# Building Q, FF and FB of a bidirectional recurrence from seven block products instead of eight

## The chip, the cores and the metric

The kernel runs on one core of a Trainium2 chip. The metric is the device time of one execution in microseconds (us), the median of several runs. The core has a matmul engine (PE, with its weight loads shown as PEld), a vector engine (DVE), an activation engine (ACT), a general engine (POOL), and SP, which here issues most of the transfers (DMAs) between DRAM and the on-chip memory (SBUF). Matmul results land in PSUM, which has 8 banks of 128 x 512 float32 values.

## What is computed

One layer of an encoder with 2048 tokens and width 1024. `h = RMSNorm(x)` is multiplied by a 1024 x 10240 matrix, whose ten column blocks of 1024 are named Q, FF, FB, I, GA, U, V, GB, MA and MB:

```
proj = h @ w_in
y_a = hgrn2(Q, FF, FB, I, GA)                    # 8 heads, chunkwise scans forward (FF) and backward (FB)
y_b = gelu(U) * (W_s @ layernorm(gelu(V)) + b) * silu(GB)
merged = sigmoid(MA) * (y_a @ w_proj_a) + sigmoid(MB) * (y_b @ w_proj_b)
out = rmsnorm(x + merged @ w_out) * final_norm_w
```

In branch A a head's state is 128 x 128. The forward scan runs over the tokens in order, the backward scan in reverse; `f = lb + (1 - lb) * sigmoid(z)` decays the state, `q = silu(Q)` reads it, `k = 1 - f` and `v = I` feed it. The two outputs are added and normalized per head.

## The kernel before

Every float32 matrix is split into two float16 parts (hi and lo) after scaling by a power of two, and one product of two such matrices is three matmuls (hi x hi, hi x lo, lo x hi) that accumulate in PSUM. There are two ways to build a projection:

- **Directly** (`mm3`, L212 to L218): for each of the 8 blocks of 128 along the inner dimension three matmuls. `proj_ch` gives 128 channels by 512 tokens (24 matmuls of 512 columns), `proj_tm` gives tokens by 256 channels (matmuls of 256 columns), `proj_wide` tokens by 512 channels. I, Q, FF, FB and V are built this way. Units of 256 columns (`halves`, L171 to L207) are loaded, squared for the scale, and split (tile `wsplit`).
- **By seven block products** (`seven`, L769; `mm12`, L821): tokens, inner dimension and channels are each cut in two, and seven products of block sums (Winograd's form of Strassen's scheme, `PRODUCTS`) replace eight. One product is 12 matmuls of 512 columns (L826). A group gives 256 channels for half of the tokens (p is the half): four tiles of 128 x 512. U, GB, MB, MA, GA and the three later projections are built this way. The weight blocks are made by `Make`: `load` (raw), `square`, `scale`, `sums` (four subtractions, L703) and `split` (four conversions on ACT, L729, and four on DVE, L730) into a tile `seven` of 1792 KB. The sums of x blocks (`x_parts`, `x_last`) go to tiles `xs`. Results leave PSUM by an ACT copy (L779) or, where a partial product is to be added, on DVE (L859).

The order of the work. `phase1` (L299) first normalizes and transposes x, 16 tiles of 128 tokens, into four tiles `xT`, with the first unit of I and the first head of Q beside it. Then it goes through the heads in pairs; for a head, first the forward scan over the four segments of 512 tokens, then the backward scan. For each segment a product of FF or FB is followed by `gla_operands` (L449: sigmoids on ACT; scans, decays and products on DVE; the scaled queries on POOL, L505), `gla_scores` (L512), `gla_states` (L563) and `gla_outputs` (L585). These four are staggered: while the products of one segment run, the scores, states and outputs of the one before are issued. The results go to DRAM (`o_d`).

`values` (L879) builds V and normalizes it. After its first products stands a branch (`tc.If`, L925) on a flag that says whether the recurrence left its numeric range; if it did, `exact` recomputes it. The sums of x blocks are made beside the remaining V products. Then `branch_b` (L998) builds U and GB and mixes positions, `merge_gates` (L1102) builds MB and MA by seven-block groups of both token halves side by side (the gate groups), `branch_a` (L1187) builds GA, and `final` (L1293) the rest. Beside the gate groups, the blocks of w_proj_a, w_out and of branch B's result are made one unit at a time in one buffer (`rt2`) and kept in DRAM. Their steps have fixed places in a list that counts products (`at`, L1162): a unit has 4 places, later 3.25, and a place is the time of one product of each of the groups that run side by side.

The framework orders the instructions of each engine by the order in the program and by when they are ready; `high_priority` moves some forward. Waits and reuse of buffers follow from the tiles: a pool with `bufs=2` gives two buffers to tiles of one name.

## Time and profile before

| | us |
|---|---|
| median of 3 runs | 2355.73 |
| lowest, highest | 2355.07, 2357.44 |
| span of the profiled execution | 2355.4 |

The profile shows one execution on the chip. Its span, from the first to the last instruction, is the time of that execution as far as the profile has it. In it the transfers moved 281.25 MB, 119 GB/s on the mean. In a table of groups, a row names the line of the kernel, the engine, the operation, the tile written and the tiles read, the shapes and the count; then busy us and the mean ns of one; then the engine's idle time just before these instructions and what ended it. In a timeline a row has start, duration, engine, line and operation, and in brackets the idle time before it. Durations of matmuls overlap, since the next begins while the last still drains.

### The profile page before, as it was taken

What the parts mean: (1) busy time and instruction counts of PE and PEld (TensorE: products, weight loads), DVE (VectorE), ACT (ScalarE), POOL (GpSimd) and SP (SyncE); (2) the same over time, 40 slices, a digit from 0 to 9 for tenths busy, and PEclk for the clock granted to TensorE, in tenths of its full rate; (3) what the DMA queues carried; (4) which work ended last, traced back from release to release, by engine and by line L of the source; (5) the groups of instructions that cost most, each with busy time, mean ns of one, the idle gap of its engine ahead of it and who ended that gap; (6) DMA issues with size and microseconds to landing.
All of it is one profiled execution on the core that took longest, in us unless ns stands there. A gap on an engine that the chain in (4) does not pass through costs nothing.

```text
span 2355.4 us, 33759 instructions
## 1 busy us (share of the span) xinstructions
PE 2311.8 (98%) x12880; PEld 1293.4 (55%) x12880; DVE 1544.7 (66%) x3033; ACT 1019.8 (43%) x1871; POOL 267.1 (11%) x507
## 2 busy tenths in 40 slices
PE   7999999999999999999999999999999999999998
PEld 5666866685668566544544554444445544444443
DVE  5686647764875587697655465677776654697754
ACT  6624333333243333433364456666565542254432
POOL 2222202220222021211000000000000000000111
PEclk9999999999999999999999999999999999999999
DMA  5201110011001000122332232576675674887643
GB/s 181 80 6 32 32 41 10 28 37 36 10 28 37 19 10 28 56 63 86 120 108 86 76 107 91 208 261 238 258 254 186 233 274 132 285 266 275 248 139 112
DMA packets 169629, 281.25 MB, mean 119 GB/s; under 512 B 10992, under 2 KB 105200, under 8 KB 162288
## 3 DMA queue, kind: packets, MB, share of 16 engines
q1 hardware_dynamic: 146272, 236.77, 30.0%
q10 hardware_dynamic: 23184, 42.22, 4.9%
q8 instruction: 104, 1.70, 0.3%
q14 instruction: 69, 0.57, 0.1%
HBM read 174.08 MB, written 104.86 MB: 118 GB/s over the span
## 4 chain that ended last, share of the span: by engine, by line
PE 51%; DVE 2%; DMA 2%; issue 1%; POOL 0%; ACT 0%; POOLq 0%; SPq 0%; DVEq 0%; ACTq 0%
PE bank L826 45%; PE pin L217 2%; PE pin L218 2%; PE pin L216 2%; PE px L1027 1%; DVE seven L730 1%; PE px L1255 1%; DMA raw<-mg 0%; DMA seven<-kept 0%; DVE tmp L649 0%; DMA zs<-ga 0%; DVE zs L859 0%; DVE zs L1467 0%; DVE zs L1445 0%; DMA out_dram<-zs 0%
## 5 line engine op out<-in xcount | busy, mean ns | idle before, releaser
L826 PEld LDWEIGHTS <-seven 128*128 128x128 f16 x5376 | 524.2, 98 | 626.1 <-issue 10.5
L826 PE MATMUL bank<-seven 128*128 128x512 f16 x2016 | 438.2, 380 | 4.8 <-DMA seven<-kept 2.1
L826 PE MATMUL bank<-xT,seven 128*128 128x512 f16 x1920 | 425.7, 379 | 0.3 <-DVE p2t L130 0.3
L826 PE MATMUL bank<-xs,seven 128*128 128x512 f16 x1440 | 320.7, 379 | 0.0
L216 PE MATMUL pin<-xT,wsplit 128*128 128x512 f16 x768 | 291.1, 379 | 0.2 <-ACT xT L281 0.2
L218 PE MATMUL pin<-xT,wsplit 128*128 128x512 f16 x768 | 291.1, 379 | 0.0
L217 PE MATMUL pin<-xT,wsplit 128*128 128x512 f16 x768 | 291.1, 379 | 0.0
L217 PE MATMUL pin<-wsplit,xT 128*128 128x256 f16 (+1 forms) x768 | 237.5, 309 | 2.4 <-DVE wsplit L205 2.1
L218 PE MATMUL pin<-wsplit,xT 128*128 128x256 f16 (+1 forms) x768 | 237.5, 309 | 2.3 <-DVE xT L282 2.0
L216 PE MATMUL pin<-wsplit,xT 128*128 128x256 f16 (+1 forms) x768 | 237.1, 309 | 0.4 <-ACT xT L281 0.4
L859 DVE SCALAR_TENSOR_TENSOR zs<-bank,us,zs 128x512 f32<-128x512 f32 x120 | 89.3, 748 | 105.2 <-PE bank L826 79.7
L779 ACT ACTIVATE zs<-bank,us 128x512 f32<-128x512 f32 x120 | 81.1, 682 | 118.1 <-PE bank L826 106.3
L867 ACT ACTIVATE zs<-zs 128x512 f32<-128x512 f32 x120 | 75.0, 625 | 121.7 <-DVE zs L859 112.5
L218 PEld LDWEIGHTS <-wsplit 128*128 128x128 f16 x768 | 75.1, 98 | 90.0 <-DVE wsplit L205 0.4
L217 PEld LDWEIGHTS <-wsplit 128*128 128x128 f16 x768 | 75.1, 98 | 77.5
L216 PEld LDWEIGHTS <-wsplit 128*128 128x128 f16 x768 | 75.3, 98 | 75.8
L505 POOL TENSOR_TENSOR q<-ff,e 128x512 f32<-128x512 f32 x64 | 71.8, 1122 | 371.6 <-DVE e L503 213.5
L730 DVE SCALAR_TENSOR_TENSOR seven<-raw,ws,seven 128x1024 f16<-128x1024 f32 x56 | 69.9, 1280 | 56.5 <-ACT seven L729 56.5
L458 ACT ACTIVATE fz<-pin,wus 128x512 f32<-128x512 f32 x64 | 43.8, 685 | 140.5 <-PE pin L218 140.3
L218 PEld LDWEIGHTS <-xT 128*128 128x128 f16 x768 | 75.4, 98 | 42.4 <-DVE xT L282 5.1
L779 ACT ACTIVATE zs<-bank,su 128x512 f32<-128x512 f32 x72 | 48.7, 680 | 112.7 <-PE bank L826 103.2
L462 DVE TENSOR_SCALAR fz<-fz,fb,fa 128x512 f32<-128x512 f32 x64 | 35.8, 559 | 93.2 <-ACT fz L458 93.2
(208 smaller groups left out, 3586.6 us busy)
## 6 DMA issues: line engine op xcount, KB each, us to landing
kept<-seven SPq DMA_DIRECT2D x16, 1792.0 KB, 8.5
seven<-kept SPq DMA_DIRECT2D x16, 1792.0 KB, 9.9
wraw<-in_w_in_dram SPq DMA_DIRECT2D x20, 1024.0 KB, 5.1
raw<-in_w_in_dram SPq DMA_DIRECT2D x40, 512.0 KB, 4.6
xt<-in_x_dram SPq DMA_DIRECT2D x16, 512.0 KB, 4.0
o_d<-ob SPq DMA_DIRECT2D x32, 256.0 KB, 2.3
v<-V SPq DMA_DIRECT2D x16, 512.0 KB, 3.5
vl<-v SPq DMA_DIRECT2D x32, 256.0 KB, 3.0
```

The costliest lines, as they stand in the source:

```text
L216: nc.tensor.matmul(ps, lh(k), rh(k), start=(k == 0), stop=False)
L217: nc.tensor.matmul(ps, lh(k), rl(k), start=False, stop=False)
L218: nc.tensor.matmul(ps, ll(k), rh(k), start=False, stop=(k == KT - 1))
L458: nc.scalar.activation(out=fz[:, 1:SEG + 1], in_=ps, func=AF.Sigmoid, scale=us)
L462: nc.vector.tensor_scalar(out=f, in0=f, scalar1=fb, scalar2=fa, op0=ALU.mult, op1=ALU.add)
L505: nc.gpsimd.tensor_tensor(out=q0.rearrange("p (m c) -> p m c", c=64), in0=ff.rearrange("p (m c) -> p m c", c=64), in1=e8.rearrange("p n b ...
L730: nc.vector.scalar_tensor_tensor(out=out[1], in0=src, scalar=s, in1=out[0], op0=ALU.mult, op1=ALU.subtract)
L779: self.reads["act"] = self.nc.scalar.activation(out=t, in_=ps, func=AF.Copy, scale=su)
L826: nc.tensor.matmul(ps, lhs(x, k), rhs(y, k), start=start and not (k or n), stop=k == 3 and n == 2, skip_group_check=True)
L859: self.reads["dve"] = self.nc.vector.scalar_tensor_tensor(out=more, in0=ps, scalar=su, in1=more, op0=ALU.mult, op1=ALU.add)
L867: self.nc.scalar.activation(out=out, in_=more, func=func)
L1027: nc.tensor.matmul(px[:, n, :], v[:, n, :], wsT[:, g, :], start=True, stop=True)
```

## The change

Q, FF and FB are built by seven-block groups. The order of the work becomes:

1. `front`: x is normalized and transposed as before. I is built in full by `proj_tm` (units 0 and 1 beside x, units 2 and 3 behind it) and stored in DRAM (`i_d`). The blocks and block sums of x are made here (`x_parts`, now with S3 too) and stored in DRAM (`x_d`, 16 blocks of 1 MB).
2. Beside the last unit of I and beside V, the blocks of 17 weight units are made (`plan_units`, `make`): Q, FF and FB in four units each, three units of MB, one each of U and GB. The subtractions run on POOL. Fifteen units go to DRAM (1792 KB each); those of Q and FF for the first pair of heads, made last, stay in SBUF.
3. `recurrence`: 24 groups for Q, FF, FB and three MB groups for token half 0 at the end, in nine phases that alternate between the halves of the tokens. Seven places in SBUF hold the blocks of x of one half; in the last group of a phase each place is refilled with the next half's block as soon as its product has read it. Weight blocks are fetched part by part. The scan work of the segments is queued and issued in steps between the products (`pump`, `step_on`). All groups use three PSUM banks.
4. The branch on the flag stands behind the recurrence, no longer inside V. Branch B begins with blocks that are in SBUF already and fetches the others; its first unit runs its groups one after the other.
5. `merge_gates` leaves out the three groups that were done in the recurrence.

Within the scan work three instructions of a segment move: f's scaling and the copy of 8 of its columns from DVE to ACT, and the product `ff * q` from DVE to POOL.

The diff, cut to its core:

```diff
-        w, U4 = self.w_in, range(4)
-        todo = []
-        for hp in U4:
-            todo += [(w, c + U * hp) for c in (C_I, C_Q, C_FF, C_FB)]
-        todo += [(w, C_V, 2), (w, C_V + 2 * U, 2)]
-        self.todo, self.made, self.hooks, self.reads = todo, [], [], {}
-        self.reads_first = True
+        w = self.w_in
+        self.todo = [(w, C_I + U * hp) for hp in range(4)] + [(w, C_V, 2), (w, C_V + 2 * U, 2)]
+        self.made, self.hooks, self.reads = [], [], {}
+        self.reads_first, self.ahead_of = True, 0
...
-    def phase1(self):
+    def front(self):
+            self.pg = E(tc.tile_pool(name="p_misc", bufs=1, space=PSUM, reuse_waits="tile"))
+            self.pin = E(tc.tile_pool(name="p_in", bufs=5, space=PSUM))
+            self.px0 = E(tc.tile_pool(name="p_x", bufs=2, space=PSUM))
+            self.wu = E(tc.tile_pool(name="wu", bufs=6))
+            self.xT = [self.xTp.tile([P, 2, 4, 2, SEG], F16, name="xT", tag="xT") for b in range(NSEG)]
+            with tc.tile_pool(name="g_i", bufs=3) as self.gi:
+                with tc.tile_pool(name="xrt", bufs=1) as self.xrt:
+                    with tc.tile_pool(name="xp", bufs=3) as self.xp, tc.tile_pool(name="nwb", bufs=2) as nwp:
+                        self.x_stage(nwp)
+                    self.i_stage(2)
+                self.rt = E(tc.tile_pool(name="rt0", bufs=3, side="right"))
+                self.plan_units()
+                self.i_stage(3)
+            self.decays()
+            self.patterns()
+            with tc.tile_pool(name="vw", bufs=3, side="right") as self.vw:
+                self.values()
...
+                self.i_pair(0, n, units[0])
+                if n == 1:
+                    units.append(self.unit(self.w_in, C_I + U, ahead=0))
+                if n >= 2:
+                    self.i_pair(1, n - 2, units[1])
+                if b >= 2:
+                    self.part(3)
+            for i, part in enumerate(((A11, A12), (A21, A22))[b % 2]):
+                nc.sync.dma_start(out=self.x_d[b // 2][part], in_=self.xT[b][:, i])
...
+        for n in range(8):
+            self.i_pair(hp, n, unit)
+            if hp == 2:
+                self.part(2)
+            else:
+                self.make(n - 9)
...
+            groups = []
+            for hp in range(4):
+                a, b = hp % 2, 1 - hp % 2
+                if hp == 0:
+                    groups.append([("q", 0, 0, 0, None), ("f", 0, 0, 1, None)])
+                groups.append([("q", hp, 1, a, ("b", hp)), ("f", hp, 1, b, ("q", hp + 1) if hp < 3 else ("mb", 0)),
+                               ("b", hp, 1, a, None)])
+                if hp < 3:
+                    groups.append([("q", hp + 1, 0, b, None), ("b", hp, 0, a, ("f", hp + 1)),
+                                   ("f", hp + 1, 0, a, None)])
+            groups.append([("b", 3, 0, 1, ("mb", 1)), ("mb", 0, 0, 0, ("mb", 2)), ("mb", 1, 0, 1, ("u", 0)),
+                           ("mb", 2, 0, 0, ("gb", 0))])
+            tail = None
+            for n, phase in enumerate(groups):
+                p, last = n % 2, n == len(groups) - 1
+                for m, (kind, hp, _, slot, after) in enumerate(phase):
+                    end = m == len(phase) - 1 and not last
+                    g = self.r_group(kind, hp, p, slot)
+                    done = partial(self.after, slot, after, p, end)
+                    if m == len(phase) - 2 and not last:
+                        self.x_fetch(1 - p, A11, self.spare)
+                    first = list(self.ORDER[:2])
+                    for i in self.ORDER[:2]:
+                        next(g)
+                        done(i)
+                        self.pump()
+                    if tail:
+                        next(tail[0])
+                        tail[1](6)
+                        self.pump()
+                    for i in self.ORDER[2:6]:
+                        next(g)
+                        done(i)
+                        self.pump()
+                    tail = g, done
+            next(tail[0])
+            tail[1](6)
+            while self.queue or any(self.pipe):
+                self.step_on(True)
+            self.X = [{c: self.slot_part(self.slot[p, c]) for c in self.PARTS} if p == 0 else {} for p in range(2)]
+            self.range_flag()
...
+    def after(self, slot, key, p, end, n):
+
+        if key and n in self.LOADS:
+            at = slice(*self.LOADS[n])
+            self.nc.sync.dma_start(out=self.ws[slot][:, :, at], in_=self.pre[key].d[:, :, at])
+        if end:
+            i = self.ORDER.index(n)
+            free = self.slot.pop((p, self.PARTS[i]))
+            if i < 6:
+                self.x_fetch(1 - p, self.PARTS[i + 1], free)
+            else:
+                self.spare = free
...
+        self.credit += 8 / 7 if ready < 5 else 3 / 2
+        while self.credit >= 1:
+            if not self.step_on(False):
+                self.credit = min(self.credit, 1.0)
+                break
+            self.credit -= 1
...
+    def step_on(self, drain):
+
+        if self.turn == 0:
+            new = None
+            if self.queue and self.queue[0]["z"] is not None:
+                new = self.queue.pop(0)
+            if new is None and not drain:
+                return False
+            if new:
+                self.operands(new)
+            if self.pipe[0]:
+                self.scores(self.pipe[0])
+            self.pipe = [new] + self.pipe
+        elif self.turn == 1:
+            g = self.pipe.pop()
+            if g:
+                self.outputs(g)
+        elif self.pipe[1]:
+            self.states(self.pipe[1])
+        self.turn = (self.turn + 1) % 3
...
-        nc.vector.tensor_scalar(out=f, in0=f, scalar1=fb, scalar2=fa, op0=ALU.mult, op1=ALU.add)
+        nc.scalar.activation(out=f, in_=kk, func=AF.Sigmoid)
         fs = self.sm.tile([P, 8], F32, name="fs")
-        lead = 0 if d == 0 else 63
-        nc.vector.tensor_copy(out=fs, in_=f[:, lead::64])
+        nc.scalar.activation(out=fs, in_=f[:, lead::64], func=AF.Identity, scale=fb, bias=fa)
...
-        nc.vector.tensor_tensor(out=ff, in0=ff, in1=q, op=ALU.mult)
+        nc.gpsimd.tensor_tensor(out=ff, in0=ff, in1=q, op=ALU.mult)
...
+        keys = [("mb", 0), ("mb", 1), ("mb", 2), ("u", 0), ("gb", 0), ("b", 0), ("b", 1), ("b", 2), ("b", 3),
+                ("q", 1), ("q", 2), ("q", 3), ("f", 1), ("f", 2), ("f", 3), ("f", 0), ("q", 0)]
+        cols = dict(mb=C_MB, u=C_U, gb=C_GB, b=C_FB, q=C_Q, f=C_FF)
+        self.pre, self.ws = {}, [None, None]
+        invs = self.c.tile([P, len(keys)], F32, name="invs")
+        for n, (kind, u) in enumerate(keys):
+            m = self.pre[kind, u] = self.make_w(self.w_in, cols[kind], u, self.rt)
+            m.to, m.adds = invs[:, n:n + 1], nc.gpsimd
+
+        def end(m, i, key):
...
+        todo = []
+        for n, w in enumerate(work):
+            todo += [(n - 1.8, w[0]), (n - 1.0, w[1]), (n, w[2]), (n + 0.8, w[3]), (n + 1.4, w[4])]
+        self.making = sorted(todo, key=lambda x: x[0])
+
+    def make(self, slot):
+
+        while self.making and self.making[0][0] <= (slot + 8) * 18 / 37 - 1.8:
+            self.making.pop(0)[1]()
+
     def values(self):
...
-        flag = self.range_flag()
-        with tc.If(flag > 0):
...
-                self.side_by_side([gate(p) for p in range(2)], slots)
+                self.side_by_side([gate(p) for p in range(2) if v > 2 or p], slots)
...
+            self.front()
+            self.recurrence()
+        flag = nc.values_load(self.flag[0:1, 0:1], min_val=0, max_val=1)
+        with tc.If(flag > 0):
+            self.exact()
```

615 lines of the change are left out of this document (358 added, 257 removed).

## Prediction, made before the changed kernel ran

> **What bounds the kernel now.** I read the page's engine shares and chain, then busy time by stage, then the groups of the stages that change.
>
> ```profile
> PE 2311.8 (98%) x12880; PEld 1293.4 (55%) x12880; DVE 1544.7 (66%) x3033; ACT 1019.8 (43%) x1871; POOL 267.1 (11%) x507
> ...
> PE 51%; DVE 2%; DMA 2%; issue 1%; POOL 0%; ACT 0%; POOLq 0%; SPq 0%; DVEq 0%; ACTq 0%
> ```
>
> PE is busy for 2311.8 of 2355.4 us, and no other engine holds over 2% of the chain. Busy time by stage follows (start:end, length, then PE, PEld, DVE, ACT and POOL busy, granted clock, DMA share, GB/s). The first row is the first 15 us of the second row's stage; then come the x blocks, the recurrence with Q, FF, FB and I, the V products, branch B, the merge gates, and the rest.
>
> ```profile
> 0.00:15.00 15.00, 3.45 (x14) 2.40 (x15) 5.47 (x16) 8.78 (x12) 4.47 (x20) 1.00 0.86 285
> ...
> 0.00:105.00 105.00, 89.27 (x651) 65.94 (x652) 61.53 (x112) 72.55 (x119) 26.72 (x66) 1.00 0.41 136
> 105.00:968.00 863.00, 851.28 (x5645) 579.75 (x5643) 596.08 (x1607) 294.77 (x694) 171.47 (x260) 1.00 0.09 28
> 968.00:1135.00 167.00, 165.51 (x782) 75.80 (x780) 120.75 (x186) 56.12 (x90) 22.79 (x44) 1.00 0.23 69
> 1135.00:1430.00 295.00, 295.00 (x1499) 150.95 (x1498) 163.54 (x250) 142.00 (x241) 3.61 (x21) 1.00 0.29 95
> 1430.00:1750.00 320.00, 319.42 (x1507) 145.06 (x1506) 223.73 (x334) 204.00 (x297) 11.26 (x32) 1.00 0.62 225
> 1750.00:2355.40 605.40, 591.33 (x2806) 275.90 (x2804) 379.04 (x546) 250.34 (x436) 31.26 (x84) 0.99 0.63 216
> ```
>
> Length less PE busy is PE's idle time: 15.7, 11.7, 1.5, 0, 0.6 and 14.1 us, together 43.6. The clock is full, so time can only come from fewer matmuls, and every new idle stretch of PE is paid in full. I sum against the span, 2355.4 us; the median of the runs, 2355.73, is 0.3 more, which I leave out.
>
> **What is removed.** Q, FF and FB are the products "pin<-xT,wsplit": 24 matmuls for each of 8 heads, 4 segments and 3 matrices, 2304 in all.
>
> ```profile
> L218 PE MATMUL pin<-xT,wsplit 128*128 128x512 f16 x768 | 291.1, 379 | 0.0
> ...
> L216 PE MATMUL pin<-xT,wsplit 128*128 128x512 f16 x768 | 291.1, 379 | 0.2 <-ACT xT L281 0.2
> ```
>
> The 379 ns overlap, so their sum is not PE's time. The spacing of starts is:
>
> ```profile
> 956.91 0.38 PE L216 MATMUL pin<-wsplit,xT 128*128 128x512 f16 x1
> ...
> 959.94 0.38 PE L218 MATMUL pin<-wsplit,xT 128*128 128x512 f16 x1
> ```
>
> Fourteen intervals in 3.03 us are 0.2164 us each. The seven-block form needs 24 groups (3 matrices, 4 column pairs, 2 token halves) of 7 products of 12 matmuls, 2016 in all. That removes 288 x 0.2164 = **62.3 us**, and PE's work becomes 2311.8 - 62.3 = 2249.5. I, V, the scans' own matmuls and the three merge-gate groups are moved, not changed in number. What remains to predict is idle time, stage by stage.
>
> **Start and x blocks.** The first product still waits for weights and the first x tiles: 15 - 3.45 = 11.6 us stay. Behind it 15.7 - 11.6 = 4.1 us were idle. The new stage adds half of the block sums (DVE and ACT, formerly beside V) while two I units instead of one I unit and a Q head run on PE, with two PSUM buffers for transposes. DVE had 61.5 and ACT 72.6 us in 105. Between 0 more and a doubling twice over (16), I take 8.
>
> **Making seventeen weight units beside I and V.** Each unit costs two ACT squares, four ACT and four DVE conversions, four subtractions (now on POOL), two loads of 512 KB and, for fifteen units, a store of 1792 KB.
>
> ```profile
> L687 ACT ACTIVATE tmp<-raw 128x1024 f16<-128x1024 f32 x56 | 58.5, 1047 | 14.3 <-DMA raw<-in_w_in_dram 11.0 <-DMA raw<-in_w_proj_b_dram 2.6 <-DMA raw<-in_w_proj_a_dram 0.7
> ...
> L729 ACT ACTIVATE seven<-raw,ws 128x1024 f16<-128x1024 f32 x56 | 61.4, 1137 | 3.4 <-DVE ws L135 3.2
> ...
> L729 ACT ACTIVATE seven<-tmp,ws 128x768 f16<-128x768 f32 x56 | 49.2, 924 | 0.0
> ...
> L505 POOL TENSOR_TENSOR q<-ff,e 128x512 f32<-128x512 f32 x64 | 71.8, 1122 | 371.6 <-DVE e L503 213.5 <-DVE ff L489 154.9 <-DVE fz L466 3.0
> ```
>
> ACT: 2 x 1.05 + 2 x 1.14 + 2 x 0.92 = 6.2 us a unit; POOL: 4 x 1.12 = 4.5. The cover is V, 768 x 0.2164 = 166 us, and the last I unit, 384 matmuls of 256 columns at half that spacing (an estimate), 42: together 208 us, 12 us a unit. The engines fit. Transfers are close: 17 x 1.05 + 15 x 1.84 MB and about 19 MB of V weights, I, V and x blocks are 64 MB, 310 GB/s.
>
> ```profile
> 1630.00:1680.00 50.00, 50.00 (x235) 22.73 (x234) 34.26 (x47) 28.26 (x39) 0.51 (x3) 1.00 0.69 258
> ...
> 2150.00:2200.00 50.00, 47.77 (x221) 21.49 (x220) 42.08 (x58) 21.09 (x38) 2.08 (x3) 1.00 0.93 330
> ```
>
> 258 GB/s cost PE nothing, 330 filled the engines to 0.93 with 2.2 us idle. The units of Q and FF that the recurrence needs first are made last, so any lag in making appears as a PE gap at the seam. Bounds: 1.5 (as V now) to 43 (64 MB at 258 GB/s take 248 us, 40 over the cover, plus a few). I take 8, nearer to the row at 330.
>
> **The recurrence.** It loses I (1152 matmuls of 256 columns in this window, 125 us) and 62 us, and gains the first Q head and three merge-gate groups (252 x 0.2164 = 54.5): 851 - 125 - 62 + 27 + 54 = 745 us of PE. Does DVE fit?
>
> ```profile
> L489 DVE TENSOR_TENSOR ff<-ff,q 128x512 f32<-128x512 f32 x64 | 44.3, 692 | 0.3
> ...
> L462 DVE TENSOR_SCALAR fz<-fz,fb,fa 128x512 f32<-128x512 f32 x64 | 35.8, 559 | 93.2 <-ACT fz L458 93.2
> L205 DVE SCALAR_TENSOR_TENSOR wsplit<-wraw,ws,wsplit 128x2048 f16<-128x2048 f32 x14 | 34.9, 2492 | 24.9 <-ACT wsplit L204 24.9
> ...
> L465 DVE COPY fs<-fz 128x8 f32<-128x8 f32 x64 | 13.0, 203 | 1.9
> ```
>
> These four groups (128 us) leave DVE: L489 goes to POOL, L462 and L465 to ACT, L205 to the front. In come the additions of partial products, three for each of 27 groups:
>
> ```profile
> L859 DVE SCALAR_TENSOR_TENSOR zs<-bank,us,zs 128x512 f32<-128x512 f32 x120 | 89.3, 748 | 105.2 <-PE bank L826 79.7 <-issue 13.3 <-PE px L737 12.0
> ```
>
> 596 - 128 + 81 x 0.748 = 529 us, 71% of 745. ACT, from 295, stays under 60%. Before, the stretches dense in scans already had DVE near 80%:
>
> ```profile
> 155.00:205.00 50.00, 50.00 (x309) 32.00 (x309) 38.48 (x103) 16.82 (x56) 15.41 (x20) 1.00 0.06 17
> 205.00:255.00 50.00, 48.82 (x309) 32.14 (x308) 39.24 (x113) 19.19 (x34) 6.87 (x13) 1.00 0.08 27
> ```
>
> There PE lost 0 and 1.2 us in 50. At that mean 745 us lose 9. Two things are worse: three product banks, whose tightest turn leaves one product (12 x 0.2164 = 2.6 us) to empty a bank, and POOL, whose instructions on two tiles double. They delay DVE:
>
> ```profile
> 172.71 0.42 DVE L560 TENSOR_TENSOR at<-at,ad 64x256 f32<-64x256 f32 x1
> ...
> 174.03 1.29 DVE L560 TENSOR_TENSOR at<-at,ad 64x256 f32<-64x256 f32 x1
> ...
> 174.00 1.04 POOL L505 TENSOR_TENSOR q<-ff,e 128x512 f32<-128x512 f32 x1 [4.85 <-DVE ff L489]
> ```
>
> The same instruction took 0.42 us alone and 1.29 beside POOL. The Trainium skill, page "SBUF — State Buffer", section "Who interferes with whom", says that a DVE instruction with two SBUF inputs and a POOL instruction that reads SBUF exclude each other for the whole instruction; these three rows agree. 64 more such meetings at 0.87 us are at most 56 us of DVE, which has 216 spare; PE sees a part. Bounds 9 to 68 (as if every meeting hit PE, 56, plus 12 as now); I take 25, because the 80% stretches already contain half of these meetings. Streaming x (8 x 7 blocks of 1 MB), weights and saved tiles is about 140 MB in 745 us, 190 GB/s, below the 258 that cost nothing. On SP's queue each fetch of an x block waits for the product that reads its place; behind it stand loads of I, of saved scores and of weight parts. Their users come three steps or a whole group (28 us with its scan work) later, so I cost this at nothing; without that cover it is one landing (5.2 us for 512 KB, below) at each of 8 changes of half, 42.
>
> **Drain and branch.** The last scan segment has no products beside it, and the branch on the range flag now stands with nothing behind it, where before V products covered it.
>
> ```profile
> 955.00:975.00 20.00, 17.58 (x120) 12.27 (x119) 14.09 (x38) 5.33 (x18) 9.64 (x11) 1.00 0.14 41
> ...
> 982.18 0.13 DVE L1493 TENSOR_SCALAR flag<-cnt 1x1 int32<-1x1 f32 x1
> ...
> 987.53 1.28 ACT L902 ACT_TABLE_LOAD   x1 [3.66 <-DVEq L925]
> ```
>
> The end of the scans cost 2.4 us with half its cover; without, I take 5 (0 to 8). From flag to ACT's first instruction behind the branch were 5.3 us, 3.7 of them waiting: I take 6 (3.7 to 10). Together 11.
>
> **Branch B and merge gates.** The first three gate steps have half the products, while making of the other weights beside them keeps its places: a place lasts 2.6 us instead of 5.2.
>
> ```profile
> L703 DVE TENSOR_TENSOR tmp<-raw 128x512 f32<-128x512 f32 x64 | 43.6, 685 | 10.6 <-ACT tmp L687 7.1 <-DMA raw<-in_w_out_dram 3.2
> ...
> raw<-in_w_proj_a_dram SPq DMA_DIRECT2D x8, 512.0 KB, 5.2
> ```
>
> One unit in its one buffer takes 5.2 us of load, 2.1 of squares, some 1.5 for the scale (an estimate), 4 x 0.685 of sums and 5 of conversions, 16 in all, against 4 x 2.6 = 10.4. Five units lag by up to 28 us; later places are 3.25 x 5.2 = 16.9 and the units there skip the squares, so they catch up. Bounds 0.6 to 28, taken with the loading of x's second half: 8.
>
> **Sum.** Idle: 11.6 + 8 + 8 + 25 + 11 + 8 + 14.1 (the end, unchanged) = 85.7. 2249.5 + 85.7 = **2335 us**, 20 less than now. Two thirds of the gain are given back at seams.
>
> **Rivals.**
> - All is hidden: old idle 43.6 plus 5 for the branch, 2298. For it: 98% busy in the old stages at equal DVE load; against it: the branch has lost its cover.
> - POOL's lock makes DVE the bound of the recurrence (slower). If all POOL work, 171 + 72 = 243 us, excludes DVE's 529, the scans need 772 us, and the first result is there only after some 11 products (29 us): 801 + 12 against 745 + 25, 43 over my sum, 2378. It decides when the recurrence idles over 25 + 20 = 45 us, 0.3 us a segment above my value. For it: the 1.29 us; against: the stretch with 38.5 us of DVE and 15.4 of POOL in 50, which kept PE at 50.00. The rule of the Trainium skill named above, taken to its end, is this case.
> - Transfers set the pace of making: 248 us instead of 208 + 8: 2367, slower too.
> - The change does nothing measurable: the give-backs reach 62. That the products are not fewer is excluded by the count above.
>
> **Chances.** My forecast (2315 to 2348) 0.50, hidden 0.20, lock 0.15, transfers 0.10, no difference 0.05. About 0.2% (4.7 us) is what a measurement can tell from no change: faster 0.70, same 0.05, slower 0.25. The range leaves out a little of the hidden case and the upper end of the lock: 2298 to 2374.
>
> **What would show it.** 288 fewer f16 matmuls of 512 columns, with Q, FF and FB on "bank"; PE idle of 20 to 30 us in that stage, with waits on DVE behind POOL; one PE gap of some 8 us between V and the recurrence, ended by a weight conversion, and one of about 11 us at the branch. Wrong would be: DVE over 90% in the recurrence, DMA share over 0.9 beside V, or no gap at the seams.

## The result and the profile after

The changed kernel takes 2374.4 us (median of 4 runs, 2370.6 to 2380.7) against 2355.4 us before (4 runs, one more than in the table above; 2355.1 to 2357.4): a ratio of 1.0079, 95% interval 1.006 to 1.0098. It is **0.8% slower** where 0.9% faster was forecast; 2374.4 lies 26 us above the forecast's 2315 to 2348 and just above the whole range, which ends at 2374. The profiled execution has a span of 2376.0 us.

Engine shares and the chain of the page of the changed kernel:

```profile
PE 2275.7 (96%) x12592; PEld 1275.6 (54%) x12592; DVE 1615.4 (68%) x2891; ACT 1158.7 (49%) x2105; POOL 447.9 (19%) x572
...
PE 19%; DMA 6%; DVE 5%; issue 3%; ACT 1%; POOL 0%; ACTq 0%; POOLq 0%; DVEq 0%; SPq 0%
```

The 288 matmuls are gone (12880 to 12592 instructions), yet PE's busy time fell by 36.1 us, not by 62.3, and PE's share of the chain fell from 51% to 19%: part of the rest now goes through DMA, DVE and issue, that is, through seams. Busy time by stage of the changed kernel follows (start:end, length, then PE, PEld, DVE, ACT, POOL busy, granted clock, DMA share, GB/s); the rows are the start, the x blocks, I and V with the making of units, the recurrence, the branch with branch B, the merge gates, the rest.

```profile
0.00:15.00 15.00, 3.53 (x14) 2.41 (x15) 5.37 (x16) 8.88 (x13) 3.49 (x16) 1.00 0.87 286
15.00:125.00 110.00, 96.20 (x835) 83.50 (x835) 92.89 (x127) 67.45 (x107) 21.88 (x34) 0.98 0.70 250
125.00:407.00 282.00, 263.54 (x1642) 157.95 (x1640) 160.71 (x233) 156.07 (x216) 119.85 (x127) 0.98 0.68 241
407.00:1169.00 762.00, 745.56 (x4532) 479.66 (x4531) 623.21 (x1435) 358.11 (x839) 249.11 (x258) 0.99 0.51 164
1169.00:1510.00 341.00, 333.17 (x1662) 167.84 (x1661) 168.31 (x260) 154.91 (x278) 10.34 (x27) 0.98 0.37 126
1510.00:1755.00 245.00, 228.15 (x1049) 101.99 (x1047) 175.51 (x264) 154.84 (x213) 11.38 (x26) 0.97 0.72 262
1755.00:2376.00 621.00, 605.52 (x2868) 282.21 (x2866) 389.38 (x559) 258.42 (x445) 31.88 (x84) 0.99 0.63 214
```

Length less PE busy is PE's idle time. The column before the DMA share is the clock, and it is below 1.00 in almost every stage; before, it was 1.00 in all but the last.

| stage | idle, forecast | idle, measured |
|---|---|---|
| start | 11.6 | 11.5 |
| x blocks | 8 | 13.8 |
| making beside I and V, with the seam | 8 | 18.5 |
| recurrence | 25 | 16.4 |
| drain and branch; branch B and merge gates | 11 + 8 | 7.8 + 16.9 |
| rest | 14.1 | 15.5 |
| **sum** | **85.7** | **100.3** |
| PE busy | 2249.5 | 2275.7 |
| span | 2335 | 2376.0 |

So the 41 us that are missing are 14.6 us of idle time and **26.2 us in which PE was busy for longer with the same matmuls**. That second part had no term in the forecast. It is seen where an idle stretch ends, in PE's timeline behind the first V products:

```profile
225.71 0.38 PE L217 MATMUL pin<-wsplit,xT 128*128 128x512 f16 x1
225.92 0.24 PE L191 MATMUL misc<-wsb,ones 128*128 128x1 bf16 x4
229.38 0.20 PE L919 MATMUL misc<-wsb,ones 128*128 128x1 bf16 x2 [3.21 <-DVE p2t L132]
233.12 1.44 PE L215 MATMUL pin<-wsplit,xT 128*128 128x512 f16 x3 [3.54 <-ACT wsplit L203]
234.36 0.63 PE L216 MATMUL pin<-wsplit,xT 128*128 128x512 f16 x1
234.78 0.63 PE L217 MATMUL pin<-wsplit,xT 128*128 128x512 f16 x1
```

Before the wait a matmul of 512 columns takes 0.38 us; after 3.21 and 3.54 us of waiting the same form takes 0.63, and starts are 0.42 us apart instead of 0.2164: half speed. Over the span the granted clock is 0.986, against 0.997 before: (1 - 0.986) x 2376.0 = 33 us of clock are withheld, before 7. The difference, 26, is the missing busy time. In the trace's record of the clock it comes in fourteen stretches at half clock, of 3.41 or 6.83 us but for the last, with 67.3 us in all; before there are three, with 12.2 us. Half of the difference is 27.5.

PE's waits in the changed kernel, by what released them (us in all, times, longest):

```profile
PE px L919 <- POOL wsb L869: 17.4, 7, 5.2
PE misc L919 <- DVE p2t L132: 11.1, 5, 5.2
PE pin L215 <- ACT xT L279: 10.0, 7, 3.0
PE pt L92 <- DVE am L90: 8.0, 1, 8.0
PE sc L713 <- POOL ff L670: 5.4, 5, 2.1
PE po L775 <- DVE fz L647: 5.2, 3, 1.7
PE bank L1009 <- PEq L1868: 4.8, 1, 4.8
```

The two longest are on L919, the matmul of one column that adds up the squares of a weight block for its scale. It stands in order in PE's queue: while its input or its bank isn't ready, no product behind it starts in these rows. The 11.1 us lie beside V, the 17.4 in the merge gates but for 2.0 in branch B. In the making, the longest of them looks like this (timeline, all engines):

```profile
325.78 4.50 DVE L912 SCALAR_TENSOR_TENSOR seven<-raw,ws,seven 128x1024 f16<-128x1024 f32 x2
...
327.07 2.12 POOL L881 TENSOR_TENSOR tmp<-raw 128x512 f32<-128x512 f32 x1
...
333.86 0.21 PE L919 MATMUL misc<-wsb,ones 128*128 128x1 bf16 x2 [5.20 <-DVE p2t L132]
```

Two conversions on DVE take 4.50 us beside a subtraction on POOL, and the tiny read that frees the scale matmul's bank stands behind them and three more on DVE, at 333.67 us. From this came two readings: that the matmul's place in the queue is the fault (**theory of the blocked queue**), or that DVE and POOL exclude each other and the making has no slack left (**the lock**). By the second, taking away one wait must bring it back at another place.

### The profile page after: what moved, and what is told of

Same layout as the page of the kernel before. It is cut to its first block, busy times and chain, and to the rows that moved or that the text cites. A ratio compares the mean times of both kernels' runs of the same rounds, so it can differ in the third digit from the quotient of the medians.

```text
span 2376.0 us, 34157 instructions
## 1 busy us (share of the span) xinstructions
PE 2275.7 (96%) x12592; PEld 1275.6 (54%) x12592; DVE 1615.4 (68%) x2891; ACT 1158.7 (49%) x2105; POOL 447.9 (19%) x572
## 5 line engine op out<-in xcount | busy, mean ns | idle before, releaser
L1009 PEld LDWEIGHTS <-seven 128*128 128x128 f16 x7392 | 725.8, 98 | 849.7 <-issue 38.4
L1009 PE MATMUL bank<-xT,seven 128*128 128x512 f16 x4116 | 939.1, 382 | 10.6 <-PEq L1868 4.8
L1043 DVE SCALAR_TENSOR_TENSOR zs<-bank,us,zs 128x512 f32<-128x512 f32 x192 | 142.1, 744 | 172.2 <-PE bank L1009 145.2
L670 POOL TENSOR_TENSOR ff<-ff,q 128x512 f32<-128x512 f32 x64 | 91.7, 1433 | 332.7 <-DVE ff L666 108.4
L865 ACT ACTIVATE tmp<-raw 128x1024 f16<-128x1024 f32 x80 | 83.8, 1048 | 67.1 <-DMA raw<-in_w_in_dram 50.0
L215 PEld LDWEIGHTS <-xT 128*128 128x128 f16 x768 | 75.8, 99 | 50.8 <-ACT xT L279 11.8
L911 ACT ACTIVATE seven<-raw,ws 128x1024 f16<-128x1024 f32 x80 | 87.7, 1137 | 31.4 <-DVE ws L137 17.0
L217 PEld LDWEIGHTS <-xT 128*128 128x128 f16 x768 | 75.8, 99 | 41.5 <-DVE xT L280 4.3
L216 PEld LDWEIGHTS <-xT 128*128 128x128 f16 x768 | 75.9, 99 | 35.5 <-issue 1.9
L760 DVE SCALAR_TENSOR_TENSOR st<-st,e,pu 128x128 f32<-128x128 f32 x240 | 82.4, 343 | 17.3 <-PE pu L752 11.6
L912 DVE SCALAR_TENSOR_TENSOR seven<-tmp,ws,seven 128x768 f16<-128x768 f32 x80 | 83.5, 1072 | 6.6 <-ACT seven L911 6.1
L1043 DVE SCALAR_TENSOR_TENSOR zs<-bank,su,zs 128x512 f32<-128x512 f32 x72 | 53.8, 747 | 48.2 <-PE bank L1009 38.3
```

The costliest lines, as they stand in the source:

```text
L215: nc.tensor.matmul(ps, lh(k), rh(k), start=(k == 0), stop=False)
L216: nc.tensor.matmul(ps, lh(k), rl(k), start=False, stop=False)
L217: nc.tensor.matmul(ps, ll(k), rh(k), start=False, stop=(k == KT - 1))
L670: nc.gpsimd.tensor_tensor(out=ff, in0=ff, in1=q, op=ALU.mult)
L760: nc.vector.scalar_tensor_tensor(out=sn, in0=st, scalar=e8[:, n, last:last + 1], in1=pu[:, n, :], op0=ALU.mult, op1=ALU.add)
L865: self.nc.scalar.activation(out=junk[:, 1024 * h:1024 * h + 1024], in_=self.raw[:, h], func=AF.Square, accum_out=self.ss[:, h:h + 1])
```

## Experiments

All times are medians beside runs of the kernel before on the same chip, and ratios are to those, with their 95% interval; the changed kernel stands at 1.0079.

### One wait at a time in the front

The constants of the decays, which include an Exp, moved ahead of the last I unit:

```diff
+                self.decays()
                 self.rt = E(tc.tile_pool(name="rt0", bufs=3, side="right"))
...
-            self.decays()
             self.patterns()
```

> Against the changed kernel (2374.4 us), the constants of the decays (one DVE-ACT-DVE chain with an Exp) are computed before the last I unit and not between I and V. Theory of the blocked queue: the wait at 226 us (6.75 us of PE idle, then 6.8 us at half clock, which cost 3.4) is the scale matmul of a weight block, which stands in PE's queue and waits for DVE, which waits for that Exp; it goes, time 8 to 10 us less, some 2365, granted clock 0.986 to 0.988. Rival of the lock (POOL's subtractions slow DVE) and rival of transfers: the wait stays with another releaser, time unchanged within 3 us.

Measured: 2373.9 us, 1.0070 (1.0056 to 1.0083). Two rows of PE's timeline of this kernel:

```profile
334.29 0.21 PE L919 MATMUL misc<-wsb,ones 128*128 128x1 bf16 x2 [6.42 <-DVE p2t L132]
...
406.96 3.60 PE L1009 MATMUL bank<-xT,seven 128*128 128x512 f16 x8 [2.61 <-DVE seven L912]
```

The gap at 226 us shrank from 6.75 to 3.4 us, and the next one, at 328, grew from 5.20 to 6.42. Two PSUM banks for the scale matmuls:

```diff
-            self.pg = E(tc.tile_pool(name="p_misc", bufs=1, space=PSUM, reuse_waits="tile"))
-            self.pin = E(tc.tile_pool(name="p_in", bufs=5, space=PSUM))
+            self.pg = E(tc.tile_pool(name="p_misc", bufs=2, space=PSUM, reuse_waits="tile"))
+            self.pin = E(tc.tile_pool(name="p_in", bufs=4, space=PSUM))
```

> Against the changed kernel, the scale matmuls of the front get two PSUM banks instead of one, and the products of I and V four instead of five. Theory of the blocked queue: the waits of the scale matmul on the reading of its bank (11.1 us on DVE L132 in the whole kernel, at 226, 328 and 347 us) go, and with them one or two stretches at half clock: 8 to 14 us less, 2360 to 2366; what stays at 226 is the wait for V's weights, about 3.5 us. Rival of the lock: DVE is late anyway, so the idle time moves to the next conversion: within 3 us of the changed kernel. Four banks for products costs under 2 us by either.

Measured: 2373.6 us, 1.0070 (1.0057 to 1.0084). The wait of L919 on p2t left the table of waits; in its place stand

```profile
PE pin L215 <- ACT wsplit L203: 5.1, 1, 5.1
...
PE misc L919 <- POOL wsb L869: 3.8, 2, 2.1
PE pin L215 <- ACT V L1117: 3.8, 1, 3.8
PE bank L1009 <- ACT seven L911: 3.8, 1, 3.8
```

which are 16.5 us; in the changed kernel the row on p2t and the rows of these names have 11.1 + 3.5 + 1.2 = 15.8. Neither edit changed the time, and both expectations of the blocked queue failed: the waits are where lateness shows, not where it arises.

### The subtractions on DVE

```diff
-            m.to, m.adds = invs[:, n:n + 1], nc.gpsimd
+            m.to = invs[:, n:n + 1]
```

> Against the changed kernel, the 68 subtractions of the seventeen units made beside I and V run on DVE instead of POOL. Rival of the lock: conversions of L912 fall back to their 1.28 us (raw) and 1.01 us (tmp), the gaps at 328 and at 402 us close: 8 to 15 us less. Theory of the blocked queue: DVE gains 68 x 0.69 = 47 us of work in a queue on which the scale matmuls wait; the conversions are shorter but stand behind the subtractions: idle time of the front the same or up to 10 us more, 2372 to 2385.

Measured: **2362.6 us, 1.0024** (1.0014 to 1.0034). The rival won. Groups of 105 to 418 us, first of the changed kernel, then of this one (count | busy, mean ns of one):

```profile
L912 DVE SCALAR_TENSOR_TENSOR seven<-raw,ws,seven 128x1024 f16<-128x1024 f32 x34 | 49.3, 1477 | 10.1 <-ACT seven L911 9.6
L881 POOL TENSOR_TENSOR tmp<-raw 128x512 f32<-128x512 f32 x34 | 48.9, 1437 | 1.5 <-DMA raw<-in_w_in_dram 0.3
```

```profile
L912 DVE SCALAR_TENSOR_TENSOR seven<-raw,ws,seven 128x1024 f16<-128x1024 f32 x34 | 42.6, 1279 | 6.2 <-ACT seven L911 6.0
...
L881 DVE TENSOR_TENSOR tmp<-raw 128x512 f32<-128x512 f32 x34 | 23.3, 687 | 17.6 <-ACT tmp L865 17.1
```

A subtraction takes 0.69 us on DVE and 1.44 on POOL, and DVE's conversions are back at 1.28. The stage from 125 to 407 us of this kernel:

```profile
125.00:407.00 282.00, 270.98 (x1690) 162.09 (x1688) 189.43 (x308) 160.19 (x220) 30.77 (x63) 0.99 0.72 254
```

DVE and POOL together held 160.7 + 119.9 = 280.6 of 282 us in the changed kernel; here it is 220. The sum of 280.6 is no sign of a lock that fills the stage: laid over each other in the trace, the two are busy at once for 63.7 us, and for 65 us neither is. What the run shows is that POOL's part in the making set its pace: the time falls by 11.8 us when DVE gets *more* work, while two edits on the waits do nothing. It does not show by which way. A subtraction on POOL takes 1.27 us with nothing on DVE beside it (26 of the 68), against 0.69 on DVE, so each unit's chain was longer by itself; and where they meet they delay each other, POOL's 68 subtractions by 11.7 us together and DVE's conversions by 11.6. The edit takes away both, and no run separates them.

### Both front edits, and the order of the first V products

The two diffs of the decays and of the subtractions, together:

> Both front edits at once: subtractions of the units on DVE and the decays before the last I unit. Each alone: 11.8 us less and nothing. Theory of the pace (beside I and V the making is paced by DVE and POOL excluding each other, so a single wait taken away comes back at the next unit): with the pace gone, the wait at 226 us is no longer given back, so its 5.9 us of idle and some 3.4 us of half clock go as well: 2353 to 2358. Rival of the blocked queue (every wait stands by itself): the sum of the two single effects, 2360 to 2363.

Measured: 2362.6 us, 1.0019 (1.0009 to 1.0030), the same as the subtractions alone. This is the range of the rival, the sum of the single effects (2360 to 2363), though both theories had counted on the wait going. The gap at 226 us stayed at 6.0 us, with waits of the same names as before: the scale of V's second weights is read on DVE behind the subtractions of a unit, and its conversion stands on ACT behind that unit's. So no step of the making was left between the first two V products:

```diff
             norm(t, 0, product(t, 0))
-            self.make(t)
         wv[1] = self.unit(self.w_in, C_V + SEG, ahead=0)
```

> Subtractions on DVE, decays early, and no step of the making between the first two V products, so that the conversion of V's second weights doesn't stand behind those of a unit on ACT and DVE. Theory: the 6 us of idle at 226 us and its 6.8 us at half clock go and, since the pace no longer binds, don't come back: 2351 to 2357. Rival (the pace still binds with 211 us of DVE): the gap moves to 393 us, the seam to the recurrence, 2360 to 2365.

Measured: 2363.6 us, 1.0031 (1.0021 to 1.0042); the gap is 5.2 us. The time is in the rival's range, but the gap didn't move to the seam with the recurrence as the rival had it: the wait there is 2.2 us with and without this edit. So the mechanism was missed by both. Subtractions of a unit begun earlier still stand on DVE ahead of V's scale. This seam isn't mended by any run here.

### Places in the merge gates

```diff
-                    at = 3 + 4 * e if e < 4 else 15 + 13 * (e - 3) // 4
+                    at = (4, 10, 16, 22, 25, 28, 30, 33, 36, 38, 41, 44, 46, 49, 52, 54)[e]
```

> Against the changed kernel, the sixteen weight and z units of the merge gates stand at places of equal time (a place beside one gate alone is half as long): 4, 10, 16, 22, 25 ... 54 instead of 3, 7, 11, 15, 18 ... 54. Theory of the blocked queue: the four waits of the scale matmul at 1514 to 1577 us (9.9 us of idle, with 3.4 us or more at half clock) go, 8 to 12 us less. Rival: the units are paced by their one buffer (14.4 to 15.6 us from conversion to conversion, 16 of them in 236 us of products), so the wait only moves to the end of the merge gates, where 6.6 us are idle now: within 3 us of the changed kernel.

Measured: 2374.1 us, 1.0075 (1.0061 to 1.0089): the rival. The waits of L919 on POOL fell from 17.4 to 7.5 us, and this stood at the end of the stage:

```profile
1757.98 2.19 ACT L911 ACTIVATE seven<-raw,wos 128x1024 f16<-128x1024 f32 x2 [7.72 <-DMA kept<-seven]
...
1762.50 5.71 PE L1009 MATMUL bank<-xs,seven 128*128 128x512 f16 x15 [8.91 <-ACT zs L962]
```

ACT waits 7.72 us until the block before is stored (1792 KB from the one buffer), and the copy that empties a product's bank stands behind it. The changed kernel shows the pace of these units in its own timeline:

```profile
1714.35 2.19 ACT L911 ACTIVATE seven<-raw,wos 128x1024 f16<-128x1024 f32 x2 [1.19 <-DMA kept<-seven]
...
1729.99 2.19 ACT L911 ACTIVATE seven<-raw,wos 128x1024 f16<-128x1024 f32 x2 [5.48 <-DMA kept<-seven]
```

These two are 15.6 us apart; over ten such steps, from 1596 to 1744 us, it is 14.8 on the mean. Sixteen units at that pace are 236 us, and the products there, 13 half gates of 84 matmuls, last 13 x 84 x 0.2164 = 236 as well. The forecast's "later units catch up" has no room to happen.

### The merge-gate groups back

```diff
...
-            groups.append([("b", 3, 0, 1, ("mb", 1)), ("mb", 0, 0, 0, ("mb", 2)), ("mb", 1, 0, 1, ("u", 0)),
-                           ("mb", 2, 0, 0, ("gb", 0))])
+            groups.append([("b", 3, 0, 1, ("u", 0))])
...
-                self.side_by_side([gate(p) for p in range(2) if v > 2 or p], slots)
+                self.side_by_side([gate(p) for p in range(2)], slots)
```

> One part of the change undone: the three merge-gate groups of the first token half go back from the end of the recurrence into the merge gates. Theory of the pace: the merge gates get back 54 us of products to cover sixteen units, so their 16.5 us of idle time and three or four stretches at half clock (6 to 8 us) go; the end of the recurrence loses its cover and idles by the scans left in the queue, 20 to 35 us; together 2370 to 2388. Rival (the idle time of the merge gates has nothing to do with cover, it is the order of the queue): merge gates idle as now, 2390 to 2410.

Measured: 2387.7 us, 1.0123 (1.0106 to 1.0140), within the range of the theory of the pace. Windows of this kernel, the end of the scans with the branch, and the merge gates:

```profile
1085.00:1162.00 77.00, 51.01 (x318) 44.39 (x318) 59.53 (x138) 27.37 (x96) 34.84 (x36) 0.82 0.21 61
...
1500.00:1800.00 300.00, 299.06 (x1413) 136.31 (x1412) 207.39 (x307) 186.08 (x260) 10.54 (x28) 1.00 0.66 242
```

The merge gates idle for 0.9 us in 300: with the old cover their idle time is gone. The end of the scans with the branch (4.6 us) idles for 26 us, at a clock of 0.82. So the groups do cover the end of the scans; but in the changed kernel the last 149 us of the recurrence are full (148.7 us of PE), which leaves the question whether two would do. With the front as in the last run on it (2363.6 us):

```diff
-            groups.append([("b", 3, 0, 1, ("mb", 1)), ("mb", 0, 0, 0, ("mb", 2)), ("mb", 1, 0, 1, ("u", 0)),
-                           ("mb", 2, 0, 0, ("gb", 0))])
+            groups.append([("b", 3, 0, 1, ("mb", 1)), ("mb", 0, 0, 0, ("gb", 0)), ("mb", 1, 0, 1, ("u", 0))])
...
-                self.side_by_side([gate(p) for p in range(2) if v > 2 or p], slots)
+                self.side_by_side([gate(p) for p in range(2) if v > 1 or p], slots)
```

> The same, and one of the three merge-gate groups (the third of the first half) back in the merge gates. Theory of cover: the merge gates get 18 us more of products, their 16 us of idle and 7 to 10 us of half clock go; the end of the recurrence keeps two groups of cover and idles 5 to 9 us, with 3 of half clock: 8 to 14 us less than the run beside it, 2340 to 2348. Rival (cover at the end of the recurrence is worth the same): no difference.

Measured: **2350.8 us, 0.9970** (0.9958 to 0.9982), 12.8 us less than without it and faster than the kernel before. The difference is as forecast; the time is above 2340 to 2348, since part of the idle time stayed. Windows of this kernel:

```profile
1120.00:1150.00 30.00, 22.23 (x152) 16.19 (x151) 18.02 (x36) 9.77 (x42) 12.50 (x15) 0.92 0.41 118
...
1480.00:1740.00 260.00, 252.82 (x1184) 114.29 (x1183) 187.19 (x279) 166.53 (x228) 10.37 (x26) 0.99 0.71 259
```

The merge gates idle for 7.2 us instead of 16.9 in the changed kernel and 17.6 in the run without this edit, and the drain and the branch together for 7.8 of 30, as the branch and what follows it did with three groups.

### Block sums of x

In the version with one group back:

```diff
                 if b >= 2:
-                    self.part(3)
+                    self.part(2)
```

> The same as the run before it, with two steps instead of three of the block sums of x after each second x tile from the third segment on; the rest of them runs beside the third I unit. If the 14 us of idle in the x blocks (9 on ACT's copies of transposes) come from the block sums on DVE and ACT: 3 to 6 us less. If they are the rhythm of the tiles themselves: no difference.

Measured: 2354.0 us, 0.9989 (0.9979 to 0.9999), no gain over the run before it; PE's wait on ACT's copies of transposes is 11.5 us instead of 10.1. A third of the steps taken away from this place changes nothing, which speaks against the sums as the cause of the idle x blocks; what the cause is stays open.

### The clock, by itself

In the kernel before, pauses of PE in branch B and the merge gates (with 1 or 5 powers):

```diff
+    def pause(self):
+        nc, pt = self.nc, self.px()
+        nc.tensor.matmul(pt[:, 0, 0:1], self.ones16, self.gapb, start=True, stop=True)
+        nc.vector.tensor_copy(out=self.gapt[:, 2:3], in_=pt[:, 0, 0:1])
+        for _ in range(5):
+            nc.gpsimd.tensor_tensor(out=self.gapt[:, 1:2], in0=self.gapt[:, 2:3], in1=self.mhalf, op=ALU.pow)
+        nc.gpsimd.tensor_copy(out=self.gapb, in_=self.gapt[:, 1:2])
+        nc.tensor.matmul(pt[:, 1, 0:1], self.ones16, self.gapb, start=True, stop=True)
```

> The kernel before (2355.7 us) with fourteen pauses of TensorE in branch B and in the merge gates, 36 us apart: a tiny matmul, a read on DVE, one power on POOL (0.88 us), a cast and a second tiny matmul that waits. Nothing else changes. Theory of the clock: a pause of 1.5 to 2 us costs its own length only, 14 x 1.8 = 25 us, 2378 to 2385, granted clock stays at 0.997. Rival (any pause slows the clock): 14 x 1.7 to 3.4 us more and a clock of 0.98.

> The same with five powers in each pause, 5 to 6 us. Theory of the clock: each pause costs its length and then 1.7 to 3.4 us at half clock (3.4 to 6.8 us of half clock each): 14 x (5.5 + 2.5) = 112, some 2467, granted clock 0.96 to 0.985. Rival (half clock is only recorded, the time after a pause is the same): 14 x 5.5 = 77, some 2433.

Measured: 2376.3 us, 1.0084 (1.0066 to 1.0101), and 2442.5 us, 1.0365 (1.0347 to 1.0383). There are sixteen pauses and not fourteen (PE has 32 instructions more, two for each), and they came out shorter than planned, about 1 and 3.2 us; so both times lie below their forecasts. For the short ones, a pause in PE's timeline and PE's share:

```profile
1242.54 0.16 PE L849 MATMUL px<-gapb,ones 128*128 128x1 bf16 x1 [1.02 <-POOL gapb L848]
```

```profile
PE 2313.2 (97%) x12912; PEld 1293.1 (54%) x12912; DVE 1541.5 (65%) x3051; ACT 1020.6 (43%) x1871; POOL 285.2 (12%) x539
```

For the long ones the same, and the two stages with pauses up to 1740 us, with fourteen of them:

```profile
1255.14 0.16 PE L849 MATMUL px<-gapb,ones 128*128 128x1 bf16 x1 [3.05 <-POOL gapb L848]
```

```profile
PE 2345.4 (96%) x12912; PEld 1303.4 (53%) x12912; DVE 1540.1 (63%) x3051; ACT 1020.3 (42%) x1871; POOL 321.7 (13%) x603
```

```profile
1135.00:1430.00 295.00, 276.07 (x1344) 138.38 (x1343) 145.07 (x228) 130.99 (x225) 22.80 (x55) 0.95 0.28 90
1430.00:1740.00 310.00, 283.95 (x1306) 128.48 (x1305) 182.76 (x290) 164.07 (x243) 37.50 (x78) 0.96 0.47 174
```

Short pauses: the span grows by 2373.2 - 2355.4 = 17.8 us, 16.4 of them idle, 1.4 busy; the clock stays at 0.999. Long pauses: the span grows by 86.7, of which 96.7 - 43.6 = 53.1 are idle and 2345.4 - 2311.8 = **33.6 are matmuls at half clock**, with a mean clock of 0.984. Had half clock been on record only, as the rival has it, the span would have grown by the 53.1 alone. Fifteen of the sixteen long pauses, of 2.7 to 3.4 us, have a stretch at half clock behind them, none of the short ones has. By sixteen, a pause of 3.2 us costs 5.4 (86.7 / 16), one of 1 us costs 1.1. The Trainium skill, page "TensorE: Matmul & The Clock Gate", section "Part 1: The HAM clock gate", says that the array falls to half its clock after an idle window of about 3.4 us and needs a busy window of that length to return; the pauses agree in kind, and they already do it at 3.05 us.

### ff x q on DVE

```diff
-        nc.gpsimd.tensor_tensor(out=ff, in0=ff, in1=q, op=ALU.mult)
+        nc.vector.tensor_tensor(out=ff, in0=ff, in1=q, op=ALU.mult)
```

> Against the changed kernel (2374.4 us), the 64 products ff x q of the scans go back from POOL to DVE; the front is left as it is. Rival of the lock in the recurrence (POOL's products slow DVE there as its subtractions did beside I and V): DVE's groups in that stage get shorter, the waits on ff and on DVE (15 us of idle with two or three stretches at half clock) shrink: 8 to 15 us less. Theory of the pace (only the making is so dense that DVE and POOL exclude each other, 305 of 313 us; the recurrence has 620 + 252 of 762 us with the overlap left over): DVE takes 64 x 0.69 = 44 us more, the waits on POOL's ff (5.4 us) go and come back as waits on DVE: within 5 us, 2369 to 2379.

Measured: 2367.9 us, 1.0040 (1.0026 to 1.0054), 6.5 us less: between the two forecasts (8 to 15 less by the lock, at most 5 by the pace). Groups of the scans, of the changed kernel and then of this one:

```profile
L670 POOL TENSOR_TENSOR ff<-ff,q 128x512 f32<-128x512 f32 x64 | 91.7, 1433 | 332.7 <-DVE ff L666 108.4 <-DVE e L684 104.5 <-DVE ff L668 61.5
L677 DVE TENSOR_TENSOR kt<-zs,w 128x256 f32<-128x256 f32 x128 | 86.5, 697 | 0.0
...
L679 DVE TENSOR_TENSOR kt<-kt,fend 128x256 f32<-128x256 f32 x64 | 38.9, 608 | 0.0
```

```profile
L677 DVE TENSOR_TENSOR kt<-zs,w 128x256 f32<-128x256 f32 x128 | 58.5, 459 | 0.0
L670 DVE TENSOR_TENSOR ff<-ff,q 128x512 f32<-128x512 f32 x64 | 45.8, 716 | 0.2
L679 DVE TENSOR_TENSOR kt<-kt,fend 128x256 f32<-128x256 f32 x64 | 31.2, 487 | 0.0
```

The product of keys that DVE issues right behind the scan takes 459 ns on the mean with ff x q on DVE and 697 with it on POOL. DVE's busy time in the whole kernel is 1598.3 us here against 1615.4, **17.1 less although it does 45.8 more**: on POOL, ff x q cost DVE 62.9 us by waiting, more than DVE needs to do it. Then the same in the version with one merge-gate group back, and q0 with it:

```diff
-        nc.gpsimd.tensor_tensor(out=q0.rearrange("p (m c) -> p m c", c=64),
+        nc.vector.tensor_tensor(out=q0.rearrange("p (m c) -> p m c", c=64),
```

> The version with one merge-gate group back (2350.8 us) and ff x q on DVE. Theory of the lock in the recurrence: the 6.5 us of the single edit come again, 2342 to 2346, DVE's busy time falls by some 17 us. Rival (the single edit's gain was a draw of half clock in the front): 2349 to 2353.

> The same and q0 = ff x e on DVE as well, so that POOL holds no large product in the recurrence. Theory of the lock: one DVE instruction waits for most of each of POOL's 64 products of 1.1 us, so POOL's saving is already paid by DVE; DVE's busy time rises by less than 20 us instead of 64 x 0.69 = 44, and the time is within 4 us of the run beside it. Rival (q0 on POOL costs DVE nothing, since it comes at the end of the operands): DVE gains 44 us, waits on ff and on q0 get longer, 5 to 15 us slower than the run beside it.

Measured: **2341.1 us, 0.9937** (0.9923 to 0.9951), and 2344.5 us, 0.9941 (0.9927 to 0.9954). The pages of the two:

```profile
PE 2263.0 (97%) x12592; PEld 1271.0 (54%) x12592; DVE 1623.5 (69%) x3023; ACT 1157.8 (50%) x2103; POOL 273.6 (12%) x440
...
PE 27%; DVE 3%; DMA 3%; issue 2%; POOL 0%; ACT 0%; ACTq 0%; SPq 0%; POOLq 0%; DVEq 0%
```

```profile
PE 2266.5 (97%) x12592; PEld 1274.5 (54%) x12592; DVE 1625.7 (69%) x3087; ACT 1158.3 (49%) x2103; POOL 198.1 (8%) x376
```

ff x q gives 9.7 us here. DVE's time falls by 18.2 us, as it did alone. q0 adds 43.7 us of work to DVE and 2.2 us to its busy time: what q0 on POOL saved DVE, DVE had lost by waiting almost in full. The time doesn't change: 3.4 us more, with intervals that overlap.

## Why the prediction was wrong, step by step

- **"The clock is full, so ... every new idle stretch of PE is paid in full."** This is the step that failed, and it decided the sign. The clock was full because PE in the kernel before, behind its start, has two waits of little over 2 us (2.21 and 2.10, each with half clock behind it) and no longer one. In the changed kernel it has thirteen, of 2.15 to 5.20 us, and half clock costs 26.2 us more than before. With the measured idle time and the old clock the span would have been 2249.5 + 100.3 = 2349.8, faster by 0.24%. The pauses put into the kernel before show the mechanism without the change: 33.6 us lost at half clock with sixteen pauses of some 3.2 us. None of the forecast's own signs of being wrong came (DVE is at 82% in the recurrence, the DMA share beside V is 0.68, the gaps at the seams are there); the clock was not among them.
- **62.3 us removed** holds. Where the clock is nearly back (the fastest version, 2341.1 us, with 2263.0 us of PE at 0.991) 13.5 us over 2249.5 are left; PE's instructions are 12592 in both.
- **Making, 8 us: mis-sized, 18.5.** The seam was forecast as one gap ended by a weight conversion. Such a gap is there, at 402 us, with 3.8 us; the others stand within V. The forecast compared ACT and POOL, each by itself, with 12 us of cover a unit; it didn't sum DVE's part and treated POOL and DVE as independent. POOL's 4 subtractions were costed at 4 x 1.12 us and took 4 x 1.44. Taking them off POOL gave 11.8 us; how much of that is POOL's own length in each unit's chain and how much its meetings with DVE stays open.
- **Transfers at 310 GB/s** were named as the danger of that stage. With the subtractions on DVE the same stage moves more, 254 GB/s instead of 241, and idles less: transfers did not set its pace.
- **Recurrence, 25 us: mis-sized, 16.4.** The price of ff x q on POOL for DVE was bounded at 56 us and is 62.9; q0, which was on POOL before, costs it 41.5 (43.7 less 2.2), and DVE is busy for 623 us there instead of 529. What PE sees of it is little, because DVE still has 139 us to spare: 6.5 to 9.7 us. The 9.7 are idle time (84.5 to 74.7 us, with PE's busy time the same within 1.5).
- **Branch and drain, 11 us: mis-sized, 4.8.** The drain costs nothing with three groups of cover. The branch costs 4.8 us, by the row of PE's waits; 6 was taken.
- **Branch B and merge gates, 8 us: mis-sized.** The two rows from the branch to 1755 us have 24.7 us of idle, the branch's 4.8 among them. The lag of 28 us was worked out rightly, but "they catch up" fails: with the store, a unit takes 14.8 us on the mean, and sixteen of them fill the 236 us of products. The undoing shows the rest: 0.9 us of idle with the old cover.
- **x blocks, 8 us: 13.8.** It is within the bounds; the cause isn't settled.
- **Rivals.** The lock gave a time of 2378, near to what came, but by another way: by it the recurrence would idle for over 45 us, and it idles for 16.4. Transfers as the pace are excluded above, all hidden by the 100.3 us, and no measurable difference by the interval, which begins at 1.006.

One thing stays open beside the x blocks and the gap at 226 us: executions of one kernel differ by more than before. The four of the changed kernel have spans of 2368.7 to 2378.8 us with clocks of 0.988 to 0.985; 0.003 x 2376 = 7 of the 10 us are clock. Why one execution draws more half clock than another was not tried.

## What to carry to other kernels

Price an idle stretch of TensorE by its length: here pauses of 1 us cost 1.1 and pauses of 3.2 us cost 5.4, so many middling gaps at seams can eat a gain that the sum of the idle times still shows. Where DVE and POOL work beside each other on SBUF, don't cost them as independent; moving a product to POOL took 63 us from DVE to save it 46. Work that moves from one stage to cover another leaves the first stage uncovered: count the periodic chains there (a load, a conversion, a store through one buffer) against the products that stay, and move only as many groups as the new place needs; of none, two and three, two were best here.

## What the runs showed of the hardware

- A pause of 3.05 us on TensorE was enough for half clock, one of 1.02 was not; 15 of 16 pauses of 2.7 to 3.4 us had it behind them. In the changed kernel the clock was at half soon after waits of 2.15 us as well, though not after each of them.
- POOL's products on two SBUF tiles delay DVE by half to two thirds of POOL's own time in this kernel: 75.7 us of q0 on POOL cost DVE 41.5, and 91.7 us of ff x q cost it 62.9. The Trainium skill, page "SBUF — State Buffer", section "Who interferes with whom", calls it an exclusive lock, and the sums agree in kind; that the loss for ff x q exceeds the work moved, 45.8 us, is what was not expected.
- PE stood for 5.20 us before a matmul of one column that is 0.19 us long, and no product behind it passed. Freeing it gained nothing here; the wait went to the next place.
